# Five seven-product pairs per unit, two of them in a row, a residual added by transfers, and turn copies in fours

## The chip, the cores and the metric

The kernel runs on one core of a Trainium2 chip. The metric is the device time of one execution in microseconds. Five engines run their own instruction queues: TensorE (PE, with its weight load PEld), VectorE (DVE), ScalarE (ACT), GpSimd (POOL) and SyncE (SP, which here issues loads). They wait for each other by semaphores. An engine runs its instructions in program order, so what stands behind a waiting instruction waits too.

## The reference

The reference is an encoder trunk in float32: 256 tokens, width 2048, two layers. The first layer's mixer is grouped-query attention, the second's a gated recurrence. Each layer ends in a SwiGLU feed-forward block, and this is what the change touches:

```python
def rms_norm(x, g):
    y = xf * lax.rsqrt(jnp.mean(xf * xf, axis=-1, keepdims=True) + EPS)
    return (y * g.astype(jnp.float32)).astype(x.dtype)

def swiglu(h, w_gate, w_up, w_down):
    return (jax.nn.silu(h @ w_gate) * (h @ w_up)) @ w_down
...
        x = x + mix
        x = x + swiglu(rms_norm(x, norm_ffn[i]), ffn_w_gate[i], ffn_w_up[i], ffn_w_down[i])
```

The hidden width of the block (D_FF) is 5632 = 44 tiles of 128.

## The kernel before

**Three matmuls per product.** Each float32 operand is split in two parts of the type float32r: `hi`, its rounded cast, and `lo`, the remainder. A product is hi·hi + lo·hi + hi·lo, three matmuls into one PSUM bank (`product`, lines 291 to 297; its matmuls are lines 293, 294 and 296). Weights come from memory in half-megabyte pieces (`raw`). ACT makes `hi` by a cast and DVE makes `lo` by a subtraction: lines 127 and 128 for a plain half, lines 145 and 148 for a seven. There are seven slots for `hi`/`lo` pairs and five for `raw`; TensorE frees a slot when it has used it.

**Units and pairs.** The FFN works in units of four hidden tiles. A unit multiplies 256 tokens by 2048 inputs and by 512 gate and 512 up columns. The 2048 inputs are eight pairs c = 0 to 7 of 256. A pair is done in one of two ways. The *plain* way (`wide`, twice) takes two halves of weights and 24 matmuls of 512 columns. The *seven* way treats the pair as a 2 by 2 block product and does it with seven products, 21 matmuls, as in Strassen's and Winograd's schemes: `load_seven` makes four sums of weights on DVE (`ws`, line 151), casts them (`ohi`, `hi`) and subtracts (`olo`, `lo`). It takes three `hi`/`lo` slots, the first for raw weights and the other two for the two tiles of sums. The products run in the order of the list at line 734: b11, b21, b22, t1, t3, t2, t4. So t1 and t3 use the first tile of sums, t2 and t4 the second. The sums of inputs on the other side (`forms`) are made once per layer by `form`, while the norm before the FFN is finished.

**Banks.** Four products of the sevens are summed over a unit in four PSUM banks (m1, p5, p7, p6, named `pm`), and four more results in accumulators c11, c21, c12 and c22 (`acc`). After the last seven (`end`) the fold adds m1, p6, p5 and p7 together (lines 741 to 745: one ACT copy and four DVE operations). At the unit's end DVE adds c11 and c21 (line 747), ACT applies SiLU (line 749, recorded as L478), DVE subtracts c12 and c22 and multiplies (lines 750, 751).

**Turning.** The result has tokens on partitions and must be turned to have features there. `turn_blocks` does a DVE transposition in blocks of 32 (line 376) and 16 copies between the blocks on ACT (line 383). Then come a cast and a remainder (lines 753, 754).

**Plan.** `SEVEN` names the pairs done the seven way in units 3 to 10 of each layer, `FEWER` those of units 0 to 2. The 44 tiles are in parts of 8, 8, 8, 8 and 12. After the first part's two units, each unit is followed by two *down* groups of the part before (the product with `w_down`, `wide_project`). A down group of eight hidden tiles is 48 matmuls. Its result, in two banks, is added to the residual stream `x_tm` by `add_residual` (line 317). The last part's down groups come at the end (`groups`).

**What sets the order.** TensorE's order is the order of the calls. The other engines' instructions are placed by a scheduler at build time, between fixed rules: `behind` chains the casts ("cast") and the DVE operations of weights ("rest") in their own order, `follow` puts one instruction after another. Once built, each engine's order is fixed.

Of the kernel before, what the change touches and what calls it, by code (L numbers as in the profile page):

```python
# [12 lines left out]
F32 = mybir.dt.float32  # L13
# [5 lines left out]
P = 128  # L19
# [9 lines left out]
UNIT = 4  # L29
SEVEN = (0, 1, 3, 5)  # L30
FEWER = {0: (0, 3, 5), 1: (1, 5), 2: (1, 5)}
# [41 lines left out]
def trunk(ctx, tc, w, out):  # L73
# [31 lines left out]

    ring, held, ft = [0], [], []

# [6 lines left out]
    def behind(key, i):  # L114
        if key in newest:
            follow(i, newest[key])
        newest[key] = i

    def load_half(src, pieces=1, then=None):
# [88 lines left out]
    def half():  # L208
        n = taken[0]
        taken[0] += 1  # L210
        if n == 0:
            return load_half(order[n], 2, partial(load_x, 0, 4))
        if n < KT // 2 and n % 2 == 0:
            load_x(2 * n, 4)
        if n == KT // 2 - 2:
            load_tables()
        got = (load_seven if isinstance(order[n], tuple) else load_half)(order[n])
        if n == KT // 2 + 1:
            follow(sync.dma_start(out=x_tm, in_=w["xt"]), newest["load"])
        g = n - KT // 2 - 2  # L220
        if 0 < g <= NW:
            follow(newest["cast"], newest["square"])
        if 0 <= g < NW:
            token_squares(g)
        return got
# [146 lines left out]

    def turn_blocks(src, engines, own=None):
        turned = tmp("one", (P, 2, WIDE), bufs=1)
        own = tmp("two", (P, 2, WIDE), bufs=1) if own is None else own
        dve.transpose(turned, src)  # L376
        t = own.rearrange("p a (b c) -> p (a b) c", c=S)
        for i in range(4):
            of = turned[32 * i : 32 * i + 32].rearrange("p a (k j c) -> p k a j c", k=4, j=4)
            for j in range(4):  # L380
                to = t[32 * j : 32 * j + 32].rearrange("p k (a i c) -> p k a i c", a=2, i=4)
                eng = engines[(4 * i + j) % len(engines)]
                (eng.copy if eng is act else eng.tensor_copy)(to[:, :, :, i, :], of[:, :, :, j, :])  # L383
        return t
# [325 lines left out]
    def ffn(norm, nxt):  # L710
        def bank():
            return ps_m.tile([P, 2 * S], F32, tag="pm", name=nm("pm"))

        def unit(seven):
            xs, r = norm.xs, [norm.r[:, a : a + 1] for a in range(2)]
            m1, p5, p7, p6 = (bank() for _ in range(4))
            c11, c21, c12, c22 = (new_acc() for _ in range(4))
# [7 lines left out]
            for c in range(KT // 2):  # L725
# [12 lines left out]
                if end:  # L738
# [5 lines left out]
                    dve.tensor_tensor(u, u, p7, ALU.add)  # L744
                    dve.tensor_tensor(x, u, p5, ALU.subtract)
            for o, y, b in ((base, base, c11), (u, u, c21)):
                dve.tensor_tensor(o, y, b, ALU.add)  # L747
            for a, (o, y, b) in enumerate(((base, v, c12), (u, x, c22))):
                table_act(o, o, AF.Silu, scale=r[a])
                dve.tensor_tensor(y, b, y, ALU.subtract)  # L750
                dve.scalar_tensor_tensor(y, y, r[a], o, ALU.mult, ALU.mult)
            t, ht = act_four(), turn_blocks(h, (act,), h)
            act.copy(t[:, :, :S], ht)
            dve.tensor_tensor(t[:, :, S:], ht, t[:, :, :S].bitcast(F32), ALU.subtract)
            return [t[:, k, :] for k in range(UNIT)]
# [3 lines left out]
        for what, i in ffn_plan():  # L759
            if what == "unit":  # L760
                hid[int(np.searchsorted(ends, i, "right"))] += unit(FEWER.get(i, SEVEN))
            else:
                add_residual(i[1], wide_project(hid[i[0]], PARTS[i[0]], bank), None)
        if nxt is not None:
# [220 lines left out]
```

## Time and profile before

| what | value |
|---|---|
| median of 3 runs | 1994.52 us (1993.63 to 1994.97) |
| the profiled execution | 1993.48 us, span 1991.6 us |
| granted TensorE clock, mean | 0.998 |
| busy, TensorE / DVE / ACT / POOL | 99% / 85% / 66% / 13% of the span |
| read from memory | 382.13 MB |

The span is the time from the first to the last recorded instruction; the execution's own time has 1.9 us more. A matmul's row shows about 0.39 us, but matmuls overlap: the step from one start to the next is what counts. In a row of groups, the figure after the second bar is the idle time of the engine just ahead of these instructions, with the instruction that ended it.

### The profile page before, as it was taken

How to read it: one execution, taken by the hardware profiler on the slowest of the kernel's cores; microseconds unless marked ns; L12 is line 12 of the kernel's file. 1: busy time of each engine (PE TensorE's matmuls, PEld its weight loads, DVE VectorE, ACT ScalarE, POOL GpSimd, SP SyncE). 2: the span in 40 equal slices, each digit the busy share in tenths (PEclk: the TensorE clock that was granted, in tenths of full speed). 3: DMA queues.
4: the chain of work that ended last, by engine and by line, in shares of the span. 5: the costliest groups of instructions: out<-in, count | busy, mean ns of one | idle time of the engine just before them, and what ended most of it. 6: DMA issues, size and time to landing. Idle time of an engine off the chain costs nothing.

```text
span 1991.6 us, 27879 instructions
## 1 busy us (share of the span) xinstructions
PE 1973.1 (99%) x9892; PEld 1679.0 (84%) x9892; DVE 1692.1 (85%) x2252; ACT 1317.3 (66%) x2033; POOL 266.6 (13%) x323
## 2 busy tenths in 40 slices
PE   9999999999999999999999999999999999999999
PEld 8888887888888888888899998878888888888887
DVE  7999789889899898987778886897898898998983
ACT  7566577666656666567688886767666666566662
POOL 0443150000000000000455450510000000000000
PEclk9999999999999999999999999999999999999999
DMA  8444646656665566656556555555566566655663
GB/s 315 160 127 127 211 140 220 218 173 203 199 236 197 175 200 207 232 194 200 192 174 194 179 171 175 193 188 207 180 233 204 171 197 207 233 200 167 207 218 131
DMA packets 108571, 386.06 MB, mean 194 GB/s; under 512 B 12176, under 2 KB 12432, under 8 KB 108304
## 3 DMA queue, kind: packets, MB, share of 16 engines
q1 hardware_dynamic: 108288, 384.26, 58.4%
q8 instruction: 78, 1.28, 0.3%
q14 instruction: 61, 0.50, 0.1%
q10 hardware_dynamic: 144, 0.02, 0.0%
HBM read 382.13 MB, written 2.10 MB: 193 GB/s over the span
## 4 chain that ended last, share of the span: by engine, by line
PE 89%; DVE 7%; POOL 1%; issue 1%; DMA 1%; ACT 1%; SPq 0%; POOLq 0%; ACTq 0%; DVEq 0%
PE acc L293 16%; PE acc L294 16%; PE acc L296 16%; PE pm L296 9%; PE pm L294 9%; PE pm L293 9%; PE acc L273 3%; PE acc L274 3%; PE acc L275 3%; DVE lo L128 2%; PE acc L262 1%; PE pm L274 1%; POOL hb L547 1%; PE pm L275 1%; PE pm L273 1%
## 5 line engine op out<-in xcount | busy, mean ns | idle before, releaser
L128 DVE TENSOR_TENSOR lo<-raw,hi 128x1024 fp32r<-128x1024 f32 (+1 forms) x549 | 672.4, 1247 | 145.9 <-ACT hi L127 140.7
L127 ACT CAST hi<-raw 128x1024 fp32r<-128x1024 f32 (+1 forms) x549 | 563.2, 1048 | 264.1 <-PE acc L294 166.2
L293 PE MATMUL acc<-hi,xg 128*128 128x512 f32 x940 | 366.7, 390 | 3.8 <-DVE one L747 3.8
L294 PE MATMUL acc<-hi,xg 128*128 128x512 f32 x940 | 366.5, 390 | 0.0
L296 PE MATMUL acc<-lo,xg 128*128 128x512 f32 x940 | 366.3, 390 | 0.0
L145 ACT CAST hi<-ws 128x1024 fp32r<-128x1024 f32 x156 | 163.5, 1053 | 237.1 <-DVE ws L151 226.3
L293 PEld LDWEIGHTS acc<-hi,xg 128*128 128x128 f32 x940 | 176.8, 188 | 41.9 <-DVE one L747 4.6
L148 DVE TENSOR_TENSOR lo<-ws,hi 128x1024 fp32r<-128x1024 f32 x156 | 190.3, 1224 | 24.8 <-ACT hi L145 22.1
L296 PEld LDWEIGHTS acc<-lo,xg 128*128 128x128 f32 x940 | 176.9, 188 | 36.9
L294 PEld LDWEIGHTS acc<-hi,xg 128*128 128x128 f32 x940 | 176.8, 188 | 36.4
L293 PE MATMUL pm<-hi,act 128*128 128x512 f32 x512 | 199.2, 389 | 0.0
L294 PE MATMUL pm<-hi,act 128*128 128x512 f32 x512 | 199.2, 389 | 0.0
L296 PE MATMUL pm<-lo,act 128*128 128x512 f32 x512 | 199.2, 389 | 0.0
L383 ACT COPY two<-one 32x256 f32<-32x256 f32 x436 | 175.9, 403 | 12.9 <-DVE one L376 7.5
L293 PE MATMUL acc<-hi,act 128*128 128x512 f32 x448 | 174.6, 390 | 0.0
L296 PE MATMUL acc<-lo,act 128*128 128x512 f32 x448 | 174.4, 389 | 0.0
L294 PE MATMUL acc<-hi,act 128*128 128x512 f32 x448 | 174.3, 389 | 0.0
L383 POOL COPY two<-one 32x256 f32<-32x256 f32 x84 | 56.6, 673 | 785.8 <-ACT form L406 646.0
L273 PE MATMUL acc<-xg,hi 128*128 128x256 f32 x512 | 145.0, 283 | 0.0
L274 PE MATMUL acc<-xg,hi 128*128 128x256 f32 x512 | 144.9, 283 | 0.0
L275 PE MATMUL acc<-xg,lo 128*128 128x256 f32 x512 | 144.7, 283 | 0.0
L262 PE MATMUL acc<-xg,hi 128*128 128x512 f32 x384 | 125.6, 398 | 1.0 <-DVE xg L398 1.0
(217 smaller groups left out, 3684.8 us busy)
## 6 DMA issues: line engine op xcount, KB each, us to landing
raw<-in_w_gate_dram SPq DMA_DIRECT2D x176, 512.0 KB, 4.4
raw<-in_w_up_dram SPq DMA_DIRECT2D x176, 512.0 KB, 3.5
raw<-in_w_down_dram SPq DMA_DIRECT2D x176, 512.0 KB, 4.7
raw<-in_w_in_dram SPq DMA_DIRECT2D x64, 512.0 KB, 4.3
raw<-in_w_qv_dram SPq DMA_DIRECT2D x40, 512.0 KB, 3.9
raw<-in_w_o_dram SPq DMA_DIRECT2D x32, 512.0 KB, 3.5
raw<-in_w_out_dram SPq DMA_DIRECT2D x32, 512.0 KB, 3.9
graw<-in_w_gates_dram SPq DMA_DIRECT2D x32, 256.0 KB, 4.1
```

The source lines that it names most:

```text
L127: behind("cast", act.copy(hi[:, sl], raw[:, sl]))
L128: behind("rest", dve.tensor_tensor(lo[:, sl], raw[:, sl], hi[:, sl].bitcast(F32), ALU.subtract))
L145: behind("cast", act.copy(hi, src))
L148: return lambda: behind("rest", dve.tensor_tensor(lo, src, hi[:].bitcast(F32), ALU.subtract))
L262: pe.matmul(acc, w, xs[k], start=(k == 0), stop=stop)
L273: pe.matmul(o, hi, x[:, :S], start=start, stop=False)
L274: pe.matmul(o, hi, x[:, S:], start=False, stop=False)
L275: pe.matmul(o, lo, x[:, :S], start=False, stop=stop)
L293: pe.matmul(o, xh, wh, start=start, stop=False)
L294: pe.matmul(o, xl, wh, start=False, stop=False)
L296: pe.matmul(o, xh, wl, start=False, stop=stop)
L383: (eng.copy if eng is act else eng.tensor_copy)(to[:, :, :, i, :], of[:, :, :, j, :])
```

## The change

Four things change.

- `SEVEN` becomes (0, 1, 3, 5, 6): units 3 to 10 do five pairs the seven way; pairs 5 and 6 are two in a row, and the fold follows pair 6. The banks are taken in the order m1, p6, p7, p5. The norm's last turn also makes the form of pair 6.
- New rules (`ahead`) on DVE's order: the fold's last subtraction stands before the fourth next operation of kind "rest"; for units 0 and 1 the add to c21 stands before the third, and the subtraction of c22 before the fourth.
- The residual of parts 0 to 3: ACT copies each bank to a tile `form` (two buffers), and POOL issues a transfer of 256 KB that adds the tile to `x_tm`. The DVE add goes.
- For units 2 to 9 (`beside`) the 16 turn copies go to a list `tail`; after the next eight halves of weights, each call of `half` issues four of them behind its casts, and then the cast and the remainder of the turned tile. Units 0, 1 and 10 keep the 16 copies together.

```diff
--- before.py
+++ after.py
@@ -27,7 +27,7 @@
 DFF = 5632
 PARTS = [8, 8, 8, 8, 12]
 UNIT = 4
-SEVEN = (0, 1, 3, 5)
+SEVEN = (0, 1, 3, 5, 6)
 FEWER = {0: (0, 3, 5), 1: (1, 5), 2: (1, 5)}
 HALF = 8
 CHUNK = HALF * P
@@ -103,7 +103,7 @@
         )
 
 
-    ring, held, ft = [0], [], []
+    ring, held, ft, ahead, tail = [0], [], [], [], []
 
     def parts(shape):
         n = ring[0] = (ring[0] + 1) % (RING + MORE)
@@ -115,6 +115,11 @@
         if key in newest:
             follow(i, newest[key])
         newest[key] = i
+        for rule in [rule for rule in ahead if key == "rest"]:
+            rule[0] -= 1
+            if rule[0] == 0:
+                follow(i, rule[1])
+                ahead.remove(rule)
 
     def load_half(src, pieces=1, then=None):
         raw = wp.tile([P, CHUNK], F32, tag="raw", name=nm("raw"), bufs=RING)
@@ -217,6 +222,8 @@
         got = (load_seven if isinstance(order[n], tuple) else load_half)(order[n])
         if n == KT // 2 + 1:
             follow(sync.dma_start(out=x_tm, in_=w["xt"]), newest["load"])
+        if tail:
+            (tail.pop(0) or list)()
         g = n - KT // 2 - 2
         if 0 < g <= NW:
             follow(newest["cast"], newest["square"])
@@ -370,17 +377,23 @@
         return pk[:, o : o + 1]
 
 
-    def turn_blocks(src, engines, own=None):
+    def turn_blocks(src, engines, own=None, spread=None):
         turned = tmp("one", (P, 2, WIDE), bufs=1)
         own = tmp("two", (P, 2, WIDE), bufs=1) if own is None else own
         dve.transpose(turned, src)
         t = own.rearrange("p a (b c) -> p (a b) c", c=S)
-        for i in range(4):
+
+        def move(i):
             of = turned[32 * i : 32 * i + 32].rearrange("p a (k j c) -> p k a j c", k=4, j=4)
             for j in range(4):
                 to = t[32 * j : 32 * j + 32].rearrange("p k (a i c) -> p k a i c", a=2, i=4)
                 eng = engines[(4 * i + j) % len(engines)]
-                (eng.copy if eng is act else eng.tensor_copy)(to[:, :, :, i, :], of[:, :, :, j, :])
+                m = (eng.copy if eng is act else eng.tensor_copy)(to[:, :, :, i, :], of[:, :, :, j, :])
+                if spread is not None:
+                    follow(m, newest["cast"])
+
+        for i in range(4):
+            move(i) if spread is None else spread.append(partial(move, i))
         return t
 
     class Norm:
@@ -711,9 +724,9 @@
         def bank():
             return ps_m.tile([P, 2 * S], F32, tag="pm", name=nm("pm"))
 
-        def unit(seven):
+        def unit(seven, later, beside):
             xs, r = norm.xs, [norm.r[:, a : a + 1] for a in range(2)]
-            m1, p5, p7, p6 = (bank() for _ in range(4))
+            m1, p6, p7, p5 = (bank() for _ in range(4))
             c11, c21, c12, c22 = (new_acc() for _ in range(4))
             new = [m1, p5, p7, p6, c11, c21, c12, c22]
 
@@ -742,25 +755,36 @@
                     dve.tensor_tensor(u, base, p6, ALU.add)
                     dve.tensor_tensor(v, u, p5, ALU.subtract)
                     dve.tensor_tensor(u, u, p7, ALU.add)
-                    dve.tensor_tensor(x, u, p5, ALU.subtract)
+                    ahead.append([4, dve.tensor_tensor(x, u, p5, ALU.subtract)])
             for o, y, b in ((base, base, c11), (u, u, c21)):
-                dve.tensor_tensor(o, y, b, ALU.add)
+                features = dve.tensor_tensor(o, y, b, ALU.add)
             for a, (o, y, b) in enumerate(((base, v, c12), (u, x, c22))):
                 table_act(o, o, AF.Silu, scale=r[a])
-                dve.tensor_tensor(y, b, y, ALU.subtract)
+                last = dve.tensor_tensor(y, b, y, ALU.subtract)
                 dve.scalar_tensor_tensor(y, y, r[a], o, ALU.mult, ALU.mult)
-            t, ht = act_four(), turn_blocks(h, (act,), h)
-            act.copy(t[:, :, :S], ht)
-            dve.tensor_tensor(t[:, :, S:], ht, t[:, :, :S].bitcast(F32), ALU.subtract)
+            if not later:
+                ahead.extend([[3, features], [4, last]])
+            if beside:
+                tail.extend([None] * PARTS[0])
+            t, ht = act_four(), turn_blocks(h, (act,), h, tail if beside else None)
+
+            def parted():
+                act.copy(t[:, :, :S], ht)
+                dve.tensor_tensor(t[:, :, S:], ht, t[:, :, :S].bitcast(F32), ALU.subtract)
+
+            tail.append(parted) if beside else parted()
             return [t[:, k, :] for k in range(UNIT)]
 
         hid = [[] for _ in PARTS]
         ends = np.cumsum(PARTS) // UNIT
         for what, i in ffn_plan():
             if what == "unit":
-                hid[int(np.searchsorted(ends, i, "right"))] += unit(FEWER.get(i, SEVEN))
+                hid[int(np.searchsorted(ends, i, "right"))] += unit(FEWER.get(i, SEVEN), i > 1, 1 < i < ends[-1] - 1)
             else:
-                add_residual(i[1], wide_project(hid[i[0]], PARTS[i[0]], bank), None)
+                for a, acc in enumerate(wide_project(hid[i[0]], PARTS[i[0]], bank)):
+                    t = tmp("form", (P, WIDE))
+                    act.copy(t, acc)
+                    pool.dma_start(out=x_tm[:, a, i[1] * WIDE : (i[1] + 1) * WIDE], in_=t, accum_op=ALU.add)
         if nxt is not None:
             ln_exp_tables()
         groups(hid[-1], PARTS[-1], PARTS[-1] - UNIT, lambda: None, partial(add_residual, norm=nxt, store=nxt is None))
```

Lines in the order below are those of each kernel: 145, 148, 151, 383, 478 before are 150, 153, 156, 391, 491 in the change; 747, 750, 751 are 760, 763, 764; 376 is 383.

First place: ACT, between unit 0 and unit 1 of the first layer. `one` and `two` hold the features of unit 0, `ws` the sums of unit 1's first seven. Before:

```order
L478 ACT_TABLE_LOAD
L478 ACTIVATE one_736_3505<-one_736_3505,nr_665_3209 128x512
L145 CAST hi_776_3678<-ws_769_3662 128x1024
L127 CAST hi_779_3705<-raw_778_3704 128x1024
L127 CAST hi_782_3723<-raw_781_3722 128x1024
L478 ACTIVATE one_736_3505<-one_736_3505,nr_665_3209 128x512
L127 CAST hi_785_3741<-raw_784_3740 128x1024
L127 CAST hi_788_3759<-raw_787_3758 128x1024
L127 CAST hi_791_3777<-raw_790_3776 128x1024
L127 CAST hi_794_3795<-raw_793_3794 128x1024
L145 CAST hi_800_3818<-raw_796_3812 128x1024
L383 COPY two_737_3506<-one_751_3593 32x8x32 x16
```

The change:

```order
L491 ACT_TABLE_LOAD
L491 ACTIVATE one_740_3517<-one_740_3517,nr_665_3209 128x512 x2
L150 CAST hi_778_3685<-ws_772_3673 128x1024
L391 COPY two_741_3518<-one_755_3605 32x8x32 x16
L150 CAST hi_780_3690<-ws_773_3674 128x1024
L132 CAST hi_783_3717<-raw_782_3716 128x1024
L132 CAST hi_786_3735<-raw_785_3734 128x1024
L132 CAST hi_789_3753<-raw_788_3752 128x1024
L132 CAST hi_792_3771<-raw_791_3770 128x1024
```

The 16 copies stood behind the eight casts shown, among them that of the second `ws` tile (hi_776). Now they stand directly ahead of the cast of the second `ws` tile (hi_780). The same holds from unit 1 to unit 2, and in the second layer.

Second place: DVE at the same point. Before:

```order
L148 TENSOR_TENSOR lo_775_3674<-ws_768_3661,hi_774_3673 128x1024
L747 TENSOR_TENSOR one_736_3505<-one_736_3505,acc_679_3253 128x512
L750 TENSOR_TENSOR two_737_3506<-acc_680_3254,two_737_3506 128x512
L750 TENSOR_TENSOR two_737_3506<-acc_681_3255,two_737_3506 128x512
L148 TENSOR_TENSOR lo_777_3679<-ws_769_3662,hi_776_3678 128x1024
L128 TENSOR_TENSOR lo_780_3706<-raw_778_3704,hi_779_3705 128x1024
L751 SCALAR_TENSOR_TENSOR two_737_3506<-two_737_3506,nr_665_3209,one_736_3505 128x512
L128 TENSOR_TENSOR lo_783_3724<-raw_781_3722,hi_782_3723 128x1024
L751 SCALAR_TENSOR_TENSOR two_737_3506<-two_737_3506,nr_665_3209,one_736_3505 128x512
L128 TENSOR_TENSOR lo_786_3742<-raw_784_3740,hi_785_3741 128x1024
L128 TENSOR_TENSOR lo_789_3760<-raw_787_3758,hi_788_3759 128x1024
L376 STREAM_TRANSPOSE one_751_3593<-two_737_3506 128x1024
```

The change:

```order
L763 TENSOR_TENSOR two_741_3518<-acc_684_3266,two_741_3518 128x512
L763 TENSOR_TENSOR two_741_3518<-acc_685_3267,two_741_3518 128x512
L156 TENSOR_TENSOR ws_772_3673<-raw_770_3669,raw_771_3670 128x512
L764 SCALAR_TENSOR_TENSOR two_741_3518<-two_741_3518,nr_665_3209,one_740_3517 128x512
L156 TENSOR_TENSOR ws_772_3673<-raw_771_3670 128x512
L153 TENSOR_TENSOR olo_777_3682<-raw_771_3670,ohi_776_3681 128x512
L764 SCALAR_TENSOR_TENSOR two_741_3518<-two_741_3518,nr_665_3209,one_740_3517 128x512
L156 TENSOR_TENSOR ws_773_3674<-ws_772_3673,raw_771_3670 128x512
L383 STREAM_TRANSPOSE one_755_3605<-two_741_3518 128x1024
L156 TENSOR_TENSOR ws_773_3674<-ws_773_3674,raw_770_3669 128x512
L153 TENSOR_TENSOR lo_779_3686<-ws_772_3673,hi_778_3685 128x1024
L153 TENSOR_TENSOR lo_781_3691<-ws_773_3674,hi_780_3690 128x1024
```

The transposition stood behind six remainders of weights; now it stands ahead of the last sum of unit 1's first seven and of the remainders of both sum tiles. The subtractions of c12 and c22 (`two<-acc,two`) and the multiplications stand between the sums.

Third place: ACT at the start of unit 3 in the change. `form` holds the residual's copy, `two_885` is the turned block of unit 2, `hi_956` to `hi_962` are casts of unit 3's second seven:

```order
L391 COPY two_885_4226<-one_899_4313 32x8x32 x4
L150 CAST hi_956_4540<-raw_952_4534 128x1024
L150 CAST ohi_958_4546<-raw_953_4535 128x512
L150 CAST hi_960_4550<-ws_954_4538 128x1024
L150 CAST hi_962_4555<-ws_955_4539 128x1024
L391 COPY two_885_4226<-one_899_4313 32x8x32 x4
L786 COPY form_930_4469<-pm_916_4395 128x512
L132 CAST hi_965_4586<-raw_964_4585 128x1024
L391 COPY two_885_4226<-one_899_4313 32x8x32 x3
L786 COPY form_931_4472<-pm_917_4396 128x512
L391 COPY two_885_4226<-one_899_4313 32x8x32
L132 CAST hi_968_4608<-raw_967_4607 128x1024
```

The turn copies go in fours between casts, and the two copies of the second down group's banks (pm_916, pm_917) stand behind and among them. Before, there were no such bank copies.

## Prediction

> **What bounds the kernel now.** I read the page first: busy times, the groups with their idle time, the chain that ended last.
>
> ```profile
> span 1991.6 us, 27879 instructions
> PE 1973.1 (99%) x9892; PEld 1679.0 (84%) x9892; DVE 1692.1 (85%) x2252; ACT 1317.3 (66%) x2033; POOL 266.6 (13%) x323
> PE 89%; DVE 7%; POOL 1%; issue 1%; DMA 1%; ACT 1%; SPq 0%; POOLq 0%; ACTq 0%; DVEq 0%
> L293 PE MATMUL acc<-hi,xg 128*128 128x512 f32 x940 | 366.7, 390 | 3.8 <-DVE one L747 3.8
> ```
>
> TensorE is busy all the time and carries 89% of the chain. Only a matmul less, or a hole in TensorE's work, can show. Of the FFN's groups only the last row has idle time that counts: 3.8 us behind DVE's L747, the add that frees an accumulator. Next the busy times of two FFN stretches and of one short window (columns: PE, PEld, DVE, ACT, POOL busy, granted clock, DMA share, GB/s).
>
> ```profile
> 300.00:900.00 600.00, 598.09 (x2637) 494.36 (x2636) 534.78 (x615) 384.75 (x510) 0.00 (x0) 1.00 0.62 205
> 1350.00:1900.00 550.00, 550.00 (x2427) 455.12 (x2426) 485.71 (x557) 351.03 (x472) 0.00 (x0) 1.00 0.60 200
> 1337.00:1341.00 4.00, 4.00 (x12) 3.14 (x11) 4.00 (x5) 2.33 (x3) 0.00 (x0) 0.57 0.29 97
> ```
>
> 550.00 / 2427 gives 0.2267 us per 512-column matmul. DVE is at 89% (534.78 / 600), ACT at 64%. So the FFN has no idle TensorE except L747's, but its two feeders run in one fixed order each, and what counts for them is where something stands, not only how much there is. The TensorE timeline shows what one wait costs:
>
> ```profile
> 1334.16 0.40 PE L296 MATMUL acc<-lo,xg 128*128 128x512 f32 x1
> 1336.41 0.50 PE L293 MATMUL acc<-hi,xg 128*128 128x512 f32 x1 [1.85 <-DVE one L747]
> 1337.21 0.58 PE L293 MATMUL acc<-hi,xg 128*128 128x512 f32 x1
> 1340.57 0.45 PE L296 MATMUL acc<-lo,xg 128*128 128x512 f32 x1
> 1340.86 0.39 PE L293 MATMUL acc<-hi,xg 128*128 128x512 f32 x1
> ...
> 321.04 0.51 PE L293 MATMUL acc<-hi,xg 128*128 128x512 f32 x1 [1.91 <-DVE one L747]
> ```
>
> The idle 1.85 us is not all. From 1337.21 to 1340.86 nine matmuls take 3.65 us in place of 9 x 0.2267 = 2.04: 1.6 us more, at a granted clock of 0.57. After the same idle at 321.04 no slow stretch came (the window 300 to 900 has clock 1.00). So of these two idles one brought it.
>
> **The change part by part.**
>
> 1. *The fifth seven-product pair.* 16 units (3 to 10, two layers) do 21 matmuls in place of 24 for pair 6: 16 x 3 x 0.2267 = 10.9 us less. This is certain, since TensorE has no other work there.
>
> 2. *The order around units 0 to 1 and 1 to 2 (both layers, four places).* The new rules put a unit's last adds and its transposition earlier on DVE, so ACT's 16 copies of the turned block come earlier. For units 0 and 1 they still are one block. In the change's ACT order that block stands between the two casts of the next seven's sums (L391 between two L150 casts), and TensorE's product p6 needs the second of these. Durations of what stands there, from DVE's and ACT's timelines and the groups:
>
> ```profile
> 317.97 0.68 DVE L745 TENSOR_TENSOR two<-one,pm 128x512 f32<-128x512 f32 x1
> 318.57 0.68 DVE L151 TENSOR_TENSOR ws<-ws,raw 128x512 f32<-128x512 f32 x1
> 319.17 1.22 DVE L148 TENSOR_TENSOR lo<-ws,hi 128x1024 fp32r<-128x1024 f32 x1
> 320.30 0.68 DVE L747 TENSOR_TENSOR one<-one,acc 128x512 f32<-128x512 f32 x1
> ...
> 324.37 0.75 DVE L751 SCALAR_TENSOR_TENSOR two<-two,nr,one 128x512 f32<-128x512 f32 x1
> 325.03 1.22 DVE L128 TENSOR_TENSOR lo<-raw,hi 128x1024 fp32r<-128x1024 f32 x1
> ...
> 329.10 1.24 DVE L376 STREAM_TRANSPOSE one<-two 128x1024 f32<-128x1024 f32 x1
> ...
> 330.84 1.05 ACT L145 CAST hi<-raw 128x1024 fp32r<-128x1024 f32 x1 [0.43 <-DMA raw<-in_w_gate_dram]
> 331.80 6.62 ACT L383 COPY two<-one 32x256 f32<-32x256 f32 x16
> 338.45 0.62 ACT L145 CAST ohi<-raw 128x512 fp32r<-128x512 f32 x1
> ```
>
> Start to start, a 512-column DVE operation takes 0.60 (317.97 to 318.57), a 1024-column one 1.13, the scale-and-multiply 0.66; a handoff to another engine costs 0.06 (320.30 + 0.68 = 320.98, TensorE starts at 321.04). Let T be the end of a unit's last matmul. The last subtraction (L750, L763 in the change) waits for it, and behind it DVE has, in the change's order: the subtraction 0.60, a sum 0.60, a multiply 0.66, a sum 0.60, the olo subtraction 0.60, a multiply 0.66, a sum 0.60, the transposition 1.24: 0.06 + 5.56 = T + 5.6. ACT then copies from T + 5.7 to T + 12.3, and the cast behind ends at T + 13.4. TensorE wants that cast after a plain pair (24 matmuls) and five products (15): T + 39 x 0.2267 = T + 8.8. It stands still for 4.6 us. Then two matmuls run (0.45), the third needs the DVE remainder, which ends 1.2 after the cast: 0.8 more. **5.4 us, four times: 21.4 us.** Without the block, the same cast would end near T + 7.4 (last sum at T + 6.2, handoff, 1.05), ahead of the 8.8; so it is the block alone that decides. In the kernel before the same block stands behind the first cast of that unit's second seven, at 331.80, and TensorE shows no idle there. After it ACT casts one tile in 0.95 against 2.72 us of TensorE's work (12 matmuls), so one wait per place is all.
>
> The slow stretch is the part I can bound only: between 0 and 1.6 us per place. One in two idles of 1.9 us brought it; these are more than twice as long, so I take two in three: 4 x 2/3 x 1.6 = 4.3 us (0 to 6.4). The Trainium skill (TensorE: Matmul & The Clock Gate, Part 1) says that the clock halves after an idle window of about 3.4 us and comes back after as long a busy one; the row at 1336.41 shows the slow stretch after less idle than that. By this rule all four places would be slow, 2.1 us more than my sum.
>
> 3. *The same rules take away L747's wait.* c21's features now stand ahead of the next seven's work on DVE and are done about 2 us before T: −3.8 us, and −1.6 for the one slow stretch.
>
> 4. *The residual.* 64 DVE adds become ACT copies and accumulating transfers from POOL's queue.
>
> ```profile
> L317 DVE TENSOR_TENSOR x<-x,pm 128x512 f32<-128x512 f32 x64 | 43.1, 684 | 40.1 <-PE pm L296 40.1
> L741 ACT COPY one<-pm 128x512 f32<-128x512 f32 x22 | 12.6, 575 | 0.0
> raw<-in_w_down_dram SPq DMA_DIRECT2D x176, 512.0 KB, 4.7
> ```
>
> DVE gives up 64 x 0.60 = 38 us and takes on 16 x (6.4 − 2.3) = 66 us (a seven: three 1.13 and five 0.60; a plain pair: two 1.13). Neither lies on TensorE's path while DVE keeps ahead. From one pair 6 (its last remainder done about 1 us before TensorE leaves the pair) to the next unit's first seven, DVE has 2.3 + 8.5 (fold and turn) + 9.0 (eight remainders) + 6.4 = 26.2 us, TensorE 5.4 + 21.8 = 27.2 before that unit, and 3.9 more to the product concerned: some 6 us of lead, of which the pairs 0 and 1 in a row take 2 x (6.4 − 4.8). A wait needs that lead gone. An accumulation of 256 KB has two buffers, so it must land within a down group, 48 x 0.2267 = 10.9 us; the nearest row is 4.7 us for 512 KB. The load from HBM shares these engines at 62%: cost 0, at most the wait of rival C. The bank copies cost something at unit 3 alone, where the second copy stands behind eleven of the turn copies: 0 to 1 us per layer, I take 0.15, 0.3 in all.
>
> 5. *Pair 6's own order.* ACT's copy of m1 waits for the pair's first product and stands ahead of its second cast: from the pair's start 0.7 + 0.57 + 1.05 + 1.2 + handoffs = 3.7, wanted after 17 matmuls, 3.85. Margin 0.15; I take 0.1 us per unit, 1.6 us (0 to 5).
>
> 6. *The form of pair 6 in the last turn of the norm.* Two ACT scalings, four POOL operations, a cast stand ahead of the sums' casts of unit 0's last seven:
>
> ```profile
> 283.29 2.15 POOL L434 TENSOR_TENSOR form<-form 128x128 f32<-128x128 f32 x2 [4.79 <-ACT form L428]
> 297.35 0.61 ACT L145 CAST ohi<-raw 128x512 fp32r<-128x512 f32 x1
> 300.58 1.05 ACT L145 CAST hi<-ws 128x1024 fp32r<-128x1024 f32 x1 [2.62 <-DVE nm L442]
> ```
>
> ACT is free at 298.0; scalings 0.9, POOL four times about 1, the cast 0.6: the sums' cast starts near 303.5 in place of 300.58. TensorE wants it near 304.5 (24 + 24 + 12 matmuls before the unit's end at 318.1), its remainder 0.45 later: cast to 304.5, remainder to 305.7, 0.8 late at most. I take 0.5 per layer, 1.0 (0 to 4).
>
> *Sum.* Profiled execution 1993.5 (span 1991.6 and 1.9 around it): −10.9 − 3.8 − 1.6 + 21.4 + 4.3 + 0.3 + 1.6 + 1.0 = 2005.8. The median of the runs, 1994.52, lies 1.0 above the profiled one: **2007 us**, 0.6% slower.
>
> **The rivals.** A difference under 0.2% (4 us) can't be told from no change.
>
> *A. The block is hidden.* If DVE reaches the transposition later than I reckon, after ACT's second cast has started, or if ACT's earlier work is late anyway, nothing is lost at the four places: 1994.5 − 16.3 + 2.9 = 1981. For it: in the kernel before the same 6.6 us is hidden entirely. Against: the order of both engines is fixed in the program; ACT can't pass the block.
>
> *B. Half a wait.* If the transposition starts about 2.5 us earlier than T + 4.4, or TensorE comes later because a load is late, the stop is 2.5 to 3 us, with few slow stretches: 1981 + 4 x 2.8 = 1992, no change. For it: handoffs I took are sums of eight durations. Against: the chain starts at TensorE's own last matmul, so both ends move together.
>
> *C. DVE's lead runs out* at pair 6 of each unit, or an accumulation lands after 10.9 us, and each of 16 units waits 1 to 2 us, on top of the forecast: 2007 + 16 to 32 = 2023 to 2039. The point from which it decides: a lead under 3 us at pair 5, DVE at 91% of a unit with two down groups (before: four sevens 25.6, four plain pairs 9.0, fold 8.5, eight remainders 9.0, four residual adds 2.4, together 54.5 us in 276 x 0.2267 = 62.6; now + 4.1 − 2.4 = 56.2 in 61.9). Against: 6 us by the reckoning in 4.
>
> **How the numbers follow.** Forecast 0.68 (own range 1999 to 2014: slow stretch 0 or all, the small terms 0 or at their ends), A 0.12, B 0.10, C 0.10. Leaving out A, a little of B and the upper part of C: 1991 to 2024. Faster by over 0.2%: A and a third of B, 0.15. Same: B's rest, 0.08. Slower: 0.77.
>
> **What would show it.** Right: four idles of 4 to 5 us of TensorE before a pm product, released by ACT's cast of the sums (L150), with the copies L391 in front of that cast; L747's successor (L760) gone from the idle; 48 matmuls less. Part 5 shows as sixteen waits of tenths on a remainder of sums; part 6 as one wait near 305 us. Wrong: no idle at these places (A), or idle spread over all units behind L153 or an accumulation (C).

## The result

The change takes 2060.78 us (median of 4 runs, 2059.55 to 2062.47), the kernel before 1994.08 beside it. The ratio is 1.0336, with a 95% interval of 1.0321 to 1.0352: 3.4% slower. The forecast was slower, but by 0.6%; the time lies outside its range.

The page of the change: the span, the busy times, the chain that ended last.

```profile
span 2057.5 us, 28141 instructions
PE 1986.0 (97%) x9844; PEld 1675.1 (81%) x9844; DVE 1724.1 (84%) x2286; ACT 1381.8 (67%) x2135; POOL 326.2 (16%) x395
PE 63%; DVE 20%; ACT 7%; issue 6%; POOL 2%; DMA 1%; DVEq 0%; ACTq 0%; SPq 0%; POOLq 0%
x<-form POOLq DMA_DIRECT2D x64, 256.0 KB, 5.5
```

The 48 matmuls are gone (9892 to 9844 rows). TensorE's share fell from 99% to 97% and its part of the chain from 89% to 63%; DVE's rose from 7% to 20%, ACT's from 1% to 7%. No engine became busy all the time: the time went into waits. The transfers land in 5.5 us, far under the 10.9 they have.

To find the waits I took, in both timelines of TensorE, each step from one 512-column matmul to the next, subtracted 0.2267 us, and added up what was over, place by place. So an idle and the slow matmuls behind it stand in one figure.

| place | before, us | change, us | forecast of the difference |
|---|---|---|---|
| 48 matmuls | | −10.9 | −10.9 |
| units 0 to 1, wait behind L747 | 6.1 | 0 | −5.4 |
| units 0 to 1 and 1 to 2, four places | 0 | 29.7 | 25.7 |
| unit 0, form of pair 6 | 0 | 3.0 | 1.0 |
| unit 3, bank copy | 0 | 2.1 | 0.3 |
| pair 6, its own order (product p6) | 0 | 0 | 1.6 |
| pairs 3 and 6 of units 4 to 10, products p5 | 0 | 31.3 | 0 |
| after unit 10, before the last groups | 0 | 14.6 | 0 |
| sum of the differences, change less before | | 63.7 | 12.3 |

The spans differ by 65.9 us; 2 us lie outside these steps.

TensorE's timeline of the change, first in unit 1's first seven (pair 1), then in pair 3 of a later unit:

```profile
327.79 0.39 PE L303 MATMUL pm<-lo,fh 128*128 128x512 f32 x1
332.96 0.51 PE L300 MATMUL pm<-hi,fh 128*128 128x512 f32 x1 [4.78 <-ACT hi L150]
334.23 0.80 PE L303 MATMUL pm<-lo,fh 128*128 128x512 f32 x1 [0.33 <-DVE lo L153]
...
647.61 0.39 PE L301 MATMUL pm<-hi,fl 128*128 128x512 f32 x1
649.58 0.50 PE L303 MATMUL pm<-lo,fh 128*128 128x512 f32 x1 [1.59 <-DVE lo L153]
```

The first is the wait forecast at the four places, released by the cast of sums (L150). The second isn't in the forecast's sum: the third matmul of product p5 waits for the remainder of the first tile of sums, in units 5 to 10 of both layers, 1.8 us each with its restart; another 0.64 follows in pair 6 of units 4 to 10. One unit with two down groups, from such a wait to the next, takes 64.36 us in place of 273 x 0.2267 = 61.9:

```profile
584.58:648.94 64.36, 62.47 (x273) 51.09 (x273) 57.67 (x67) 43.21 (x59) 3.49 (x4) 1.00 0.69 212
```

DVE is busy 57.67 of 64.36, 90%, and ACT 67%. Neither is full. The clock is 1.00, so this is waiting alone.

### The profile page after: what moved, and what is told of

The parts are those of the page before. It is cut to its first block, busy times and chain, and to the rows that moved or that the text cites. A ratio compares the mean times of both kernels' runs of the same rounds, so it can differ in the third digit from the quotient of the medians.

```text
span 2057.5 us, 28141 instructions
## 1 busy us (share of the span) xinstructions
PE 1986.0 (97%) x9844; PEld 1675.1 (81%) x9844; DVE 1724.1 (84%) x2286; ACT 1381.8 (67%) x2135; POOL 326.2 (16%) x395
## 4 chain that ended last, share of the span: by engine, by line
PE 63%; DVE 20%; ACT 7%; issue 6%; POOL 2%; DMA 1%; DVEq 0%; ACTq 0%; SPq 0%; POOLq 0%
PE acc L301 9%; PE acc L300 9%; PE acc L303 9%; PE pm L303 8%; PE pm L300 8%; PE pm L301 8%; DVE ws L156 5%; DVE lo L133 4%; DVE lo L153 4%; ACT two L391 3%; PE acc L280 3%; PE acc L281 3%; PE acc L282 3%; ACT hi L150 2%; DVE olo L153 1%
## 5 line engine op out<-in xcount | busy, mean ns | idle before, releaser
L133 DVE TENSOR_TENSOR lo<-raw,hi 128x1024 fp32r<-128x1024 f32 (+1 forms) x517 | 630.8, 1248 | 151.3 <-ACT hi L132 136.6
L132 ACT CAST hi<-raw 128x1024 fp32r<-128x1024 f32 (+1 forms) x517 | 527.5, 1047 | 218.3 <-DMA raw<-in_w_down_dram 83.8
L150 ACT CAST hi<-ws 128x1024 fp32r<-128x1024 f32 x188 | 197.6, 1053 | 246.2 <-DVE ws L156 233.2
L300 PE MATMUL acc<-hi,xg 128*128 128x512 f32 x844 | 331.1, 392 | 0.0
L301 PE MATMUL acc<-hi,xg 128*128 128x512 f32 x844 | 330.5, 392 | 0.0
L303 PE MATMUL acc<-lo,xg 128*128 128x512 f32 x844 | 330.3, 391 | 0.0
L153 DVE TENSOR_TENSOR lo<-ws,hi 128x1024 fp32r<-128x1024 f32 x188 | 229.7, 1224 | 32.0 <-ACT hi L150 27.9
L787 POOL DMA_DIRECT2D x<-form x64 | 56.0, 989 | 1118.8 <-ACT form L786 1118.8
L301 PEld LDWEIGHTS acc<-hi,xg 128*128 128x128 f32 x844 | 160.1, 190 | 33.8
L300 PEld LDWEIGHTS acc<-hi,xg 128*128 128x128 f32 x844 | 160.2, 190 | 33.2
L303 PEld LDWEIGHTS acc<-lo,xg 128*128 128x128 f32 x844 | 159.8, 189 | 33.6
L153 DVE TENSOR_TENSOR lo<-raw,hi 128x1024 fp32r<-128x1024 f32 x94 | 114.8, 1221 | 48.2 <-ACT hi L150 45.1
```

Of the source, the lines that this page charges most:

```text
L132: behind("cast", act.copy(hi[:, sl], raw[:, sl]))
L133: behind("rest", dve.tensor_tensor(lo[:, sl], raw[:, sl], hi[:, sl].bitcast(F32), ALU.subtract))
L150: behind("cast", act.copy(hi, src))
L153: return lambda: behind("rest", dve.tensor_tensor(lo, src, hi[:].bitcast(F32), ALU.subtract))
L300: pe.matmul(o, xh, wh, start=start, stop=False)
L301: pe.matmul(o, xl, wh, start=False, stop=False)
```

## The experiments

Theory: ACT's copies do harm by where they stand, between a tile of sums, its cast and its remainder, because DVE and ACT pass each seven to and fro. Rival 1: DVE's work with five sevens is too much wherever the copies stand. Rival 2: the bank copies and transfers cost the time.

**Rules off for units 0 and 1**

```diff
-            if not later:
+            if False:
                 ahead.extend([[3, features], [4, last]])
```

> The change with the two DVE rules for units 0 and 1 left out (features before the third, last subtraction before the fourth operation on weights). In its ACT order the block of 16 copies stands behind the casts of unit 1's pair 2 again, not ahead of the cast of the second tile of sums. Theory (the block is what costs at these four places): the idles of 4.5 to 4.8 us and the slow stretches behind them go, 29.6 us by the step times of TensorE's timeline, and the wait for c21's add comes back, about 6 us: 2061 - 29.6 + 6 = 2037 us. Rival (fold and sums together are too much for DVE there, wherever the copies are): the idles stay, released by a remainder, 2055 to 2061.

Measured: 2031.25 us, ratio 1.0189 (1.0159 to 1.0219), 6 us under the expectation. All four idles are gone (29.7 us); at unit 0 to 1 a wait behind the add to c21 returned, 2.0 us in each layer, less than the 3 us of the kernel before. The other places are as in the change: 31.4 us in pairs 3 and 6, 13.4 before the last groups. So with the rules the four places take 29.7 us and that wait takes 4.0 us less, and the later waits do not come from them.

In the change, ACT's timeline at this place shows the block between the two casts of sums, and DVE's what it does meanwhile:

```profile
322.28 1.05 ACT L150 CAST hi<-ws 128x1024 fp32r<-128x1024 f32 x1 [3.53 <-DVE ws L156]
325.23 6.62 ACT L391 COPY two<-one 32x256 f32<-32x256 f32 x16 [1.89 <-DVE one L383]
331.87 1.04 ACT L150 CAST hi<-ws 128x1024 fp32r<-128x1024 f32 x1
```

```profile
323.96 1.23 DVE L383 STREAM_TRANSPOSE one<-two 128x1024 f32<-128x1024 f32 x1
325.12 0.65 DVE L156 TENSOR_TENSOR ws<-ws,raw 128x512 f32<-128x512 f32 x1
332.94 1.23 DVE L153 TENSOR_TENSOR lo<-ws,hi 128x1024 fp32r<-128x1024 f32 x1 [6.04 <-ACT hi L150]
```

The second sums are ready at 325.8. ACT takes up their cast at 331.87, after the 6.62 us of copies that stand ahead of it in ACT's order. The copies themselves had waited for the transposition, which ended at 325.2.

**Fours for units 0 and 1 too**

```diff
-hid[...] += unit(FEWER.get(i, SEVEN), i > 1, 1 < i < ends[-1] - 1)
+hid[...] += unit(FEWER.get(i, SEVEN), i > 1, i < ends[-1] - 1)
```

> The change with the copies of units 0 and 1 in fours too (on the list that is issued from the ninth call after the unit on), rules as in the change. Theory (the block's place decides at the four places): the idles of 4.8 us and their slow stretches go, 29.6 us; the waits of units 3 to 10 stay: 2061 - 29.6 = 2031. Fours then stand in units 1 and 2 between casts, where only two sevens stand: 0 to 2 us per place. Rival (early transposition and adds on DVE hold up the sums, wherever the copies are): idles of 2 to 4 us stay, 2045 or more.

Measured: 2038.89 us, 1.0225 (1.0206 to 1.0243). The four idles are gone with the rules still in, which rules out that early adds on DVE hold up the sums by that much. Missed by 8 us: 3.5 to 4 us per layer of smaller waits in units 1 to 3 take their place (one for a remainder, up to 373.7, 1.24 us idle, is the longest), unit 4 waits 1.8 us at p5 in place of 0.4, and two of the later waits brought a slow stretch of 1.9 us each.

**Copies in one block in all units**

```diff
-hid[...] += unit(FEWER.get(i, SEVEN), i > 1, 1 < i < ends[-1] - 1)
+hid[...] += unit(FEWER.get(i, SEVEN), i > 1, False)
```

> The change with all units' copies in one block (nothing on the list that is issued behind later casts). In its ACT order the block then stands ahead of a cast of sums in units 2 to 9 as well. Theory (it is the copies' place between sums and their casts that costs, the fours in a milder form): an idle of up to 4.8 us per unit in place of 2.4, between 2061 and 2061 + 16 x 3 = 2110. Rival (the fours themselves cost the 2.4 us per unit, a block would be hidden as it was before): 2061 - 31 = 2030.

Measured: 2052.08 us, 1.0293 (1.0259 to 1.0328), below the theory's range and far above the rival's. In six units of each layer the block costs about what the fours cost, 2.0 us (3.7 and 2.3 in two of the twelve). ACT's timeline (698 is in pair 0 of a unit):

```profile
688.67 6.63 ACT L391 COPY two<-one 32x256 f32<-32x256 f32 x16 [0.64 <-DVE one L383]
695.33 1.05 ACT L150 CAST hi<-ws 128x1024 fp32r<-128x1024 f32 x1
...
697.75 0.58 ACT L786 COPY form<-pm 128x512 f32<-128x512 f32 x1
...
699.18 0.58 ACT L786 COPY form<-pm 128x512 f32<-128x512 f32 x1
```

TensorE waited here for the two bank copies (L786), 0.47 us each, and later 0.26 for a remainder: the block held up what stood behind it, whichever that was. So neither the theory nor the rival had it: putting the copies together doesn't free the chain, and it isn't dearer than the fours either. Why it costs 2.0 us here and 7.4 at units 0 and 1 was not tried apart.

**Four sevens, all else as in the change**

```diff
-SEVEN = (0, 1, 3, 5, 6)
+SEVEN = (0, 1, 3, 5)
```

> The change with pairs 0, 1, 3 and 5 as before, no seven in pair 6: rules, transfers, fours as in the change. Theory (fours of copies use up the lead, and the fifth seven has none left to give): the waits in pairs 3 and 6 of units 3 to 10 (31 us) shrink to under 0.5 us per unit, the wait at the form of pair 6 (3 us) goes, the four places keep theirs: 1994 + 29.6 - 6 + 2 to 10 = 2020 to 2028. Rival (fours or transfers cost 2 us per unit by themselves): 2048 or more.

Measured: 2036.24 us, 1.0214 (1.0184 to 1.0244). The waits behind DVE in units 3 to 10 are all gone, and those of pair 6's form and of the last groups too. But it is 8 us above the expectation: a wait of 1.04 us stands in each of 16 units, at product p6 of pair 0, behind a bank copy. In ACT's and TensorE's timelines:

```profile
567.78 1.23 ACT L391 COPY two<-one 32x256 f32<-32x256 f32 x3
569.04 0.59 ACT L786 COPY form<-pm 128x512 f32<-128x512 f32 x1
```

```profile
569.68 0.50 PE L300 MATMUL pm<-hi,fh 128*128 128x512 f32 x1 [0.77 <-ACT form L786]
```

That is the wait which the change has at unit 3 only, here in every unit. So the fours cost with four sevens too, in another place; and with five, DVE's later sums are what is late. This run alone doesn't separate theory from rival 1, as it takes 4.1 us of DVE's work out of each unit.

**Copies of units 2 to 9 on POOL**

```diff
-            if beside:
-                tail.extend([None] * PARTS[0])
-            t, ht = act_four(), turn_blocks(h, (act,), h, tail if beside else None)
+            t, ht = act_four(), turn_blocks(h, (pool,) if beside else (act,), h)
+            if beside:
+                tail.extend([None] * (PARTS[0] + 4))
```

> The change with the 16 copies of units 2 to 9 on POOL, right behind the transposition, and not on ACT in fours; the cast and remainder of the turned tile stay at their place behind the twelfth half. POOL takes 16 x 0.67 = 10.8 us and is idle there. Theory (ACT's copies between casts hold up DVE, which stood idle 1.4 to 1.5 us four times per unit behind ACT's casts): the waits of 1.8 and 0.6 us per unit go, 2061 - 31 = 2030. Rival (DVE's work with five sevens is too much, 91% of a unit): the waits stay, 2055 to 2065. Second rival (POOL's copies slow DVE, 0.95 in place of 0.69 us as at 284 us in the profile before): 10.8 x 0.38 = 4 us of DVE per unit, half of the gain at most.

Measured: 2035.62 us, 1.0211 (1.0181 to 1.0241), 6 us above the expectation. This separates theory from rival 1. In units 4 to 10 no wait is left in pairs 3 and 6, with the same sevens, the same DVE operations and the same transfers. A window of 62 us in these units (columns as before: PE, PEld, DVE, ACT, POOL):

```profile
700.00:762.00 62.00, 62.00 (x275) 51.36 (x274) 60.33 (x67) 36.65 (x43) 19.77 (x21) 1.00 0.70 222
```

DVE is at 97% and TensorE never waits. At 90% in the change it did. So DVE's share was not the matter. POOL's copies do slow DVE's operations, as the second rival has it (last section), but no wait of TensorE's comes of it in these units. What the fours did is seen in the change's ACT timeline, from pair 0's second cast of sums to pair 3's first cast:

```profile
625.45 1.05 ACT L150 CAST hi<-ws 128x1024 fp32r<-128x1024 f32 x1 [2.00 <-DVE ws L156]
626.41 1.64 ACT L391 COPY two<-one 32x256 f32<-32x256 f32 x4
628.08 1.05 ACT L150 CAST hi<-raw 128x1024 fp32r<-128x1024 f32 x1
...
634.63 1.66 ACT L391 COPY two<-one 32x256 f32<-32x256 f32 x4
636.31 1.05 ACT L132 CAST hi<-raw 128x1024 fp32r<-128x1024 f32 x1
637.39 1.65 ACT L391 COPY two<-one 32x256 f32<-32x256 f32 x4
639.07 1.05 ACT L132 CAST hi<-raw 128x1024 fp32r<-128x1024 f32 x1
640.15 1.65 ACT L391 COPY two<-one 32x256 f32<-32x256 f32 x4
641.82 1.05 ACT L150 CAST hi<-raw 128x1024 fp32r<-128x1024 f32 x1
```

and in DVE's:

```profile
629.16 1.22 DVE L153 TENSOR_TENSOR lo<-raw,hi 128x1024 fp32r<-128x1024 f32 x1 [1.40 <-ACT hi L150]
...
637.40 1.23 DVE L133 TENSOR_TENSOR lo<-raw,hi 128x1024 fp32r<-128x1024 f32 x1 [1.53 <-ACT hi L132]
640.15 1.23 DVE L133 TENSOR_TENSOR lo<-raw,hi 128x1024 fp32r<-128x1024 f32 x1 [1.53 <-ACT hi L132]
642.90 1.23 DVE L153 TENSOR_TENSOR lo<-raw,hi 128x1024 fp32r<-128x1024 f32 x1 [1.52 <-ACT hi L150]
...
645.85 1.22 DVE L773 TENSOR_TENSOR act<-two,act 128x1024 fp32r<-128x1024 f32 x1
646.98 1.41 DVE L156 TENSOR_TENSOR ws<-ws,raw 128x512 f32<-128x512 f32 x2
648.31 2.48 DVE L153 TENSOR_TENSOR lo<-ws,hi 128x1024 fp32r<-128x1024 f32 x2
```

From 634.6 to 642 ACT does nothing but four copies, a cast, four copies, a cast. A cast comes every 2.76 us, and TensorE uses up a half in 12 x 0.2267 = 2.72. So in the plain pair 2, where DVE should gain on TensorE, ACT lets it gain nothing. From pair 1's first remainder to pair 3's, DVE stands idle four times, 1.40 + 1.53 + 1.53 + 1.52 = 6.0 us. Then in pair 3 the turned tile's remainder (L773, at 645.85) and both second sums stand ahead of the first sums' remainder, which ends at 649.5: TensorE starts at 649.58.

What POOL's copies left: 8 to 10 us at unit 3 per layer, behind bank copies, and 4.0 behind the add to c21 after unit 10. The wait before the last groups for the cast of the turned tile is gone, though unit 10's copies are still on ACT. DVE's transposition starts 8.6 and 8.9 us after the unit's last matmul here, and 14.1 and 13.5 us after it in the change (3.3 in the kernel before). So DVE is less late here, and the wait goes with that. But this run alone doesn't show that the one made the other, since the stop of 4.0 us gives the tile time too; a run below without that stop (all copies on POOL, transfers) keeps 1.6 us of the wait. In the change the unit's matmuls end near 930, DVE transposes at 944.75 behind the remainders of the groups' weights, and the cast that TensorE waits for from 952.6 on ends at 955.7:

```profile
944.75 1.24 DVE L383 STREAM_TRANSPOSE one<-two 128x1024 f32<-128x1024 f32 x1
```

```profile
946.11 6.63 ACT L391 COPY two<-one 32x256 f32<-32x256 f32 x16
...
954.66 1.04 ACT L772 CAST act<-two 128x1024 fp32r<-128x1024 f32 x1
```

**The fifth seven alone**

```diff
# on the kernel before
-SEVEN = (0, 1, 3, 5)
+SEVEN = (0, 1, 3, 5, 6)
```

> The kernel before with the seven in pair 6 and nothing else (residual on DVE, no rules, copies in one block). In its ACT order the block of 16 copies stands, in most of units 3 to 9, right behind the first cast of the next unit's first sevens and ahead of the casts of sums, where before it stood behind casts of a later plain pair. Theory (the place of the copies decides): 2 to 4 us of idle per unit: 1994 - 11 + 3 (form of pair 6) + 16 x 2 to 4 = 2018 to 2050. Rival (five sevens are fine by themselves, rules, fours and transfers brought the loss): 1984 to 1990.

Measured: 2027.07 us, 1.0163 (1.0134 to 1.0193), within the theory's range and 37 us or more above the rival's, but not as the theory had it, in every unit. Without rules, fours and transfers the fifth seven turns 10.9 us less work into 33 us more time. Seven of the sixteen units 3 to 10 of the two layers have a wait of 1.6 to 2.3 us for a remainder, most with a slow stretch behind. ACT's timeline ahead of one, and below it the block ahead of a unit that has no such wait:

```profile
737.74 1.06 ACT L145 CAST hi<-ws 128x1024 fp32r<-128x1024 f32 x1 [2.29 <-DVE ws L151]
741.88 6.64 ACT L383 COPY two<-one 32x256 f32<-32x256 f32 x16 [3.08 <-DVE one L376]
748.54 1.05 ACT L145 CAST hi<-ws 128x1024 fp32r<-128x1024 f32 x1
```

```profile
679.13 0.61 ACT L145 CAST ohi<-raw 128x512 fp32r<-128x512 f32 x1
679.65 6.63 ACT L383 COPY two<-one 32x256 f32<-32x256 f32 x16
```

In the first the block stands between the same two casts as at units 0 to 1 of the change, the casts of the first seven's two tiles of sums. The trace has fourteen such blocks, those that turn units 3 to 9 in both layers. Seven stand between these two casts, and exactly these are followed by the seven waits. The other seven stand behind the `ohi` cast of the second seven, as some did in the kernel before, and none has such a wait. The work per unit is the same in both kinds, so the wait goes with the place, and not with how much ACT or DVE has to do.

**The residual by transfers alone**

```diff
# on the kernel before
-                add_residual(i[1], wide_project(hid[i[0]], PARTS[i[0]], bank), None)
+                for a, acc in enumerate(wide_project(hid[i[0]], PARTS[i[0]], bank)):
+                    t = tmp("form", (P, WIDE))
+                    act.copy(t, acc)
+                    pool.dma_start(out=x_tm[:, a, ...], in_=t, accum_op=ALU.add)
```

> The kernel before with the residual of parts 0 to 3 by bank copies on ACT and accumulating transfers from POOL's queue, nothing else. Theory (transfers cost nothing unless copies stand ahead of the bank copies): 1990 to 1996. Rival (each down group's bank is freed later than by DVE's add, 1.04 us per unit as with four sevens in the change): 2005 to 2012.

Measured: 1995.70 us, 1.0009 (0.9998 to 1.0020): no change that can be told, as expected. Rival 2 falls for bank copies and transfers by themselves; behind turn copies a bank copy does cost time, as the run with four sevens shows. It also shows that 38 us less DVE work gain nothing by themselves.

**All copies of units 0 to 9 on POOL, with either residual**

Both have the rules for units 0 and 1, the rule for c21's add for unit 10, and pair 6's form cast behind the first half of unit 0's pair 6.

> The change with the turn copies of units 0 to 9 on POOL, the residual by DVE's add as before, the rule for the add to c21 for units 0, 1 and 10 (that for c22 for 0 and 1), and the cast and remainder of pair 6's form behind the first half of unit 0's pair 6. No copies of ACT stand between sums' casts of units 0 to 9. Theory (place of ACT's copies): TensorE's idles go but for tenths: 1994 - 10.9 - 6 + 0 to 4 = 1977 to 1981. Rival (DVE's work: 2.4 us of residual adds per unit more than in the change, 95% of a unit): waits of 1 to 2 us per unit, 1993 to 2010.

> The same as the run with all copies on POOL and DVE's residual, but the residual by bank copies and transfers as in the change. Units 4 to 10 without waits as with POOL's copies in units 2 to 9 alone. At unit 3 the transfers stand behind three blocks of copies on POOL's queue, and a third bank copy waits for the first transfer's landing: about 10 us per layer as in that run, 1978 + 20 = 1998. If the copies of unit 2 are done before the first transfer is issued, nothing: 1978.

Measured: 1994.15 us with DVE's residual, 0.9998 (0.9987 to 1.0009); 2000.16 with transfers, 1.0028 (1.0013 to 1.0044). The waits at units 0 to 1, 1 to 2 and unit 0's form are gone in both (0.4 to 0.6 us per layer left). With DVE's residual the time is in the rival's range, but the rival's waits of 1 to 2 us per unit aren't there. Two other things were missed: in five units of each layer 0.46 us, 0.6 to 1.3 in three of these ten, behind the residual add, and 5.5 to 6.1 us per layer before the last groups. With transfers units 4 to 10 have no wait, 1.6 us per layer stand before the last groups, and unit 3 has the 9 to 10 us that were forecast. POOL's queue and ACT's there:

```profile
410.54 15.95 POOL L391 COPY two<-one 32x256 f32<-32x256 f32 x16 [26.63 <-DVE one L383]
426.43 1.91 POOL L797 DMA_DIRECT2D x<-form  x2
```

```profile
430.55 0.59 ACT L796 COPY form<-pm 128x512 f32<-128x512 f32 x1 [2.40 <-DMA x<-form]
```

The transfers stand behind unit 2's copies, and the third bank copy needs the first one's buffer.

**A mixed version, and unit 10**

Residual by DVE for the two down groups after unit 2, by transfers for the others; all copies on POOL; both rules for units 0, 1 and 10; pair 6's form cast late, as in the two runs above. The second run has DVE's residual everywhere. The third is the mixed one with unit 10's copies shared by ACT and POOL and its cast one half earlier:

```diff
# on the change
...
-            if not later:
+            if later < 2 or later == 10:          # later is now the unit's number
                 ahead.extend([[3, features], [4, last]])
-            if beside:
-                tail.extend([None] * PARTS[0])
-            t, ht = act_four(), turn_blocks(h, (act,), h, tail if beside else None)
+            t, ht = act_four(), turn_blocks(h, (pool,) if later < 10 else (act, pool), h)
+            tail.extend([None] * (PARTS[0] + 4 if later < 10 else 6))
...
+                if i[0] == 0 and i[1] < 2:
+                    add_residual(i[1], wide_project(hid[i[0]], PARTS[i[0]], bank), None)
+                    continue
```

> All units' turn copies on POOL (unit 10 too, its cast and remainder behind the eighth half of the last groups), the rules for c21 and c22 for units 0, 1 and 10, the cast of pair 6's form behind the first half of unit 0's pair 6, residual by DVE for the two down groups after unit 2 and by bank copies and transfers for all others. Theory (ACT's copies in the chain of sums, casts and remainders made the loss; transfers behind three blocks of POOL's copies made unit 3's wait; unit 10's block made the wait before the last groups): only tenths of idle stay in the FFN, 1994.5 - 10.9 - 6 + 1 to 4 = 1978 to 1982. Rival (unit 10's tile is late on POOL too, 10.8 us of copies in place of 6.6): 1984 to 1990.

> The same with the residual by DVE in all down groups. Theory: the 0.46 us per unit behind DVE's residual add stays (14 units, 6.5 us), the 11.5 us before the last groups go: 1994 - 11 = 1983, 1982 to 1987, behind the mixed one by 3 to 6 us. Rival (the residual's place doesn't matter): equal to the mixed one.

> The mixed version with unit 10's 16 copies shared by ACT and POOL (eight each) and its cast and remainder behind the seventh half of the last groups. POOL's part ends 6 us earlier. Theory: the 4.9 us before the last groups (twice) go, 1989 - 9.8 = 1979, at least 1983. Rival (ACT's eight copies hold up the casts of the last groups): an idle of 1 to 3 us per layer in another place, 1983 to 1987.

Measured: mixed 1989.03 us, 0.9973 (0.9961 to 0.9984); with DVE's residual 1999.56, 1.0030 (1.0020 to 1.0041); mixed with shared copies **1979.64, 0.9927 (0.9914 to 0.9941)**, 0.7% faster than the kernel before. In the first the units have no wait above 0.6 us, but the last groups wait 4.7 to 5.0 us per layer: the rival came true. DVE, POOL and ACT there:

```profile
906.67 1.23 DVE L383 STREAM_TRANSPOSE one<-two 128x1024 f32<-128x1024 f32 x1
```

```profile
908.03 12.51 POOL L391 COPY two<-one 32x256 f32<-32x256 f32 x16 [40.24 <-DVE one L383]
```

```profile
920.76 1.04 ACT L780 CAST act<-two 128x1024 fp32r<-128x1024 f32 x1
```

In the second this wait is 8.1 to 8.6 us, which I had not expected: the run missed its range by 12 us. Its trace shows DVE's transposition 11.2 us after unit 10's last matmul, in the first run 8.6, and 13.5 us for POOL's 16 copies in place of 12.5, together 3.6 us more. The 0.46 us came in ten units, not in 14. In the third run the wait is gone. Its waits in the FFN come to 1.0 us (6.1 in the kernel before), and its page reads:

```profile
span 1977.7 us, 28155 instructions
PE 1960.5 (99%) x9844; PEld 1669.8 (84%) x9844; DVE 1780.1 (90%) x2294; ACT 1237.5 (63%) x1791; POOL 653.2 (33%) x723
```

So the fifth seven can pay its 10.9 us once the copies, the transfers and the form stand where nobody waits behind them. The gain is 14.0 us, and waits of some 5 us that the kernel before had are gone too. No run has these places with four sevens, so what they give without the fifth was not measured.

## Why the prediction was wrong

Its side was right and its size wrong: +12.3 us forecast, +67 measured.

*Part 1* held: 48 matmuls, 10.9 us.

*Part 2* held, and its mechanism is shown by two runs (rules off, fours at units 0 and 1). The idle was reckoned at 4.6 us and is 4.54 to 4.81. Its slow stretch came four times in four, not two in three: 7.4 us per place in place of 6.4.

*Part 3* held: that wait is gone, 6.1 us for 5.4.

*Part 4* is the step that failed: "Neither lies on TensorE's path while DVE keeps ahead", with "some 6 us of lead". The sum of DVE's operations came close (56.2 us per unit reckoned, 57.67 busy). What it left out is that DVE's remainders wait for ACT's casts, and that the 16 copies stood in fours ahead of four of these casts; the order rows of the third place showed them. They held DVE up by 6.0 us, as much as the lead. Rival C named the symptom, "DVE's lead runs out", and its price of 1 to 2 us per unit (measured 2.4 with the restarts in units 5 to 10, mostly in pair 3 and not in pair 6), but put it down to DVE's share of a unit, 91%, and gave it one chance in ten. POOL's copies show that at 97% DVE still feeds TensorE. The bank copy at unit 3, taken at 0.15 us, is 1.0, the upper end of its bounds. The transfers by themselves did cost nothing.

*Part 5* was not seen at product p6: pair 6 waits at p5, 0.37 us, for the first tile's remainder, and the second is then in time.

*Part 6* had the right place and the bound: 0.78 us idle (reckoned at most 0.8; I took 0.5), 1.4 to 1.6 with the restart.

*Missing from the sum*: unit 10, 14.6 us. The sum has no term for the way from unit 10 to the last groups, and its copies are one block before and after. But its fold now follows pair 6, one seven later, and DVE came there without a lead: the transposition starts 14 us after the unit's end, where it was 3.3. With four sevens and all else as in the change it is 5.7 us, and nothing waits.

*Rivals A and B* fell: nothing at the four places is hidden or halved.

The clock rule of the Trainium skill (TensorE: Matmul & The Clock Gate, Part 1), an idle window of about 3.4 us, came out better than my two in three here: all four idles of over 4.5 us brought a slow stretch, and none of the twelve of 1.5 to 1.6 us in the change did. It isn't strict, though: two idles of 3.18 and 3.36 us before the last groups brought one, in the run with fours at units 0 and 1 two of 1.82 and 1.88 us did, and the kernel before had one after 1.85.

## What to carry to other kernels

Where two engines hand work to and fro, add up the chain across both, with all that stands between the handoffs on either queue; the busy share of each alone said nothing on the lead here (DVE fell behind at 90% and did not at 97%). A filler of 1.6 us behind every 1 us cast was not hidden here, because filler and cast together did not stay under the consumer's step (2.76 against 2.72 us left nothing to catch up with). After making one pair cheaper on the bound engine, look at the stage's ends too: here the last unit before another stage lost more than the pairs saved.

## What the runs showed of the hardware that I had not expected

POOL's copies took 0.67 us each on the mean in the kernel before, but up to 16.84 us for 16, 1.05 each, beside a busy DVE. DVE's operations with two inputs took longer in turn while they ran. POOL's row, and DVE's for the same subtraction during the copies and after their end at 644.2, in the run with POOL's copies:

```profile
627.38 16.84 POOL L391 COPY two<-one 32x256 f32<-32x256 f32 x16
```

```profile
633.98 0.88 DVE L153 TENSOR_TENSOR olo<-raw,ohi 128x512 fp32r<-128x512 f32 x1
...
644.68 0.68 DVE L153 TENSOR_TENSOR olo<-raw,ohi 128x512 fp32r<-128x512 f32 x1
```

The Trainium skill (SBUF — State Buffer, Who interferes with whom) says that a DVE instruction with two SBUF inputs contends with a GpSimd instruction that reads SBUF; these rows agree, and give the price: 0.20 us on 0.68. The second rival of that run had reckoned with 0.95 in place of 0.69. The price was worth paying here, since no wait of TensorE's came of it in units 4 to 10.
